# Splitting h later, loading h behind the weights, and adding the down evictions on VectorE: one step of a hybrid encoder layer

## The chip, the cores and the metric

The kernel runs on one core of a Trainium2 chip. The metric is the device time of one execution in microseconds, the median of the runs shown. A core has TensorE (PE; PEld is its weight load), VectorE (DVE), ScalarE (ACT), GpSimd (POOL) and SyncE (SP); DMAs are issued from the queues of SP, ACT and POOL and run on 16 DMA engines that these share.

## The reference

One encoder layer for a prompt of 512 frames with 16 meta tokens and for a decode step of 64 frames; from the residual on, 512 + 64 = 576 tokens are computed together. Width 2048, hidden width of the feed-forward part 5632, all in float32:

```python
h = h + concat([pool_mixer(u), diff_attention(q, k, v)]) @ w_out     # u, q, k, v = rmsnorm(h) @ w_in
n = rmsnorm(h, g_ffn)
h = h + (silu(n @ w_gate) * (n @ w_up)) @ w_down                     # the part that the change touches
y = rmsnorm(h, g_final)
```

## The kernel before

Activations are kept transposed, features on the 128 partitions and tokens along the free dimension. Every float32 matmul is made of three: each operand is split into a high part in float32r (a ScalarE copy) and a low part (a VectorE subtraction of the high part from the original), and high x high, high x low and low x high are accumulated (L808 to L810).

**Seven products.** Gate, up and down are done in blocks of two by two (two halves of the features in, two of the features out, or of the tokens: TN = 288), with seven products in place of eight. An object of class `Seven` holds one such step: `load` brings four raw weight blocks on SP's queue (L786), `prep(i)` forms the i-th combination of them on VectorE (L793 to L797) and splits it (L837, L838 for gate and up; L1070, L1071 for down), `product(i)` runs its matmuls into one of three PSUM banks A, B, C and calls the eviction. Several products use one bank after another: a bank's second product continues to accumulate on the first, so it must wait until the first one's eviction has read the bank. `run` (L814) traces, ahead of each product, the preparation of the product three steps later.

**Gate and up.** There are 22 pairs f, each a gate step and an up step of 7 x 8 x 3 = 168 matmuls. `inner` evicts (L864 to L880): ScalarE copies the first product out, VectorE adds the others; the last gate product accumulates into bank B, whose earlier content L873 reads at i = 4. After the last up product (i = 6) GpSimd forms the combinations of h that the down products need (L908 to L911). Then h[f], seven blocks of 128 x 288, is split in two portions, blocks 0 to 3 and 4 to 6: hi by ScalarE (L917, one buffer in tag "xlast"), the low part by VectorE in place (L918), hi stored to DRAM by a DMA from POOL's queue after each portion (L919), and the low part stored for all seven blocks at once (L920). The last f is stored whole and not split (L913).

**Down.** 40 turns: five passes r of eight output tiles m, each turn one `Seven` over up to five f's (2 to 5 in the first pass, 5 in the middle ones, 5 to 2 in the last). Products go in the order 1, 0, 2, 4, 3, 5, 6. The h of an f comes back in four loads (f, q) on SP's queue (L988): q = 0, 1, 2 are pairs of blocks (tile hc), q = 3 is the seventh block (tile hh). The weights of turns 0 and 1 (EARLY = 2) come early, those of turn 2 are loaded by `down[EARLY].load()`. After each product `hooks` takes one load from a list in order of f and q if a place is free. Loads of f >= 3 that are taken in turns 0 and 1 are ordered behind turn 2's weights with `issue_after`, which sets an order within one queue and no wait. `down_evac` evicts a product into y or a1 in SBUF: in pass 0 mostly by a ScalarE copy; later products 0, 3 and 6 by a ScalarE copy to a tile ev (L1087) and a DMA from POOL's queue that adds ev to its target (L1088), the others by a VectorE addition (L1090).

**What sets the order.** The tile framework traces the program and then a planner writes each engine's queue, by its own costs of the instructions; an engine works its queue strictly in that order. `issue_after` is how the program asks for an order. Tiles of one tag share their buffers in turn.

Of the kernel before, what the change touches and what calls it, by code (L numbers as in the profile page):

```python
# [11 lines left out]
F32 = mybir.dt.float32  # L12
F32R = mybir.dt.float32r
AF = mybir.ActivationFunctionType
ALU = mybir.AluOpType
# [4 lines left out]
P = 128  # L20
# [30 lines left out]
def hymba_step(  # L51
# [6 lines left out]
    nc = tc.nc  # L58
# [476 lines left out]
    for h in range(HEADS):  # L535
        hd = Head(h)
# [138 lines left out]
    TN = NQ // 2  # L675
# [3 lines left out]
    fs = ffb.enter_context(tc.tile_pool(name="fs", bufs=1, reuse_waits="tile"))  # L679
# [173 lines left out]
    hd = [dram.tile([P, 7, 2 if j < FT // 2 - 1 else 1, TN], F32, name=f"hd{j}") for j in range(FT // 2)]  # L853

    def inner(s, i, out, scale):


        A, B, C = s.b
        tt = nc.vector.tensor_tensor
        o11, o12, o21, o22, o2 = out  # L860
        if i == 0:
            pu = fs.tile([P, 2, TN], F32, name="pu", tag="acc")
            s.p1, s.u2 = pu[:, 0], pu[:, 1]
            nc.scalar.activation(s.p1, A, AF.Copy)  # L864
        elif i == 1:
            tt(s.u2, B, s.p1, op=ALU.add)
        elif i == 2:
            s.t5 = fs.tile([P, TN], F32, name="t5", tag="pre")
            tt(s.t5, C, s.p1, op=ALU.add)
        elif i == 3:  # L870
            tt(o11, A, scale[:, 0, 0], op=ALU.mult)
        elif i == 4:
            tt(o22, B, s.t5, op=ALU.add)  # L873
        elif i == 5:
            tt(o12, C, s.u2, op=ALU.add)
        else:
            tt(o21, B, s.p1, op=ALU.add)
        if i == 6:
            nc.gpsimd.tensor_tensor(o12, o12, scale[:, 0, 1], op=ALU.mult)
            nc.gpsimd.tensor_tensor(o2, o2, scale[:, 1], op=ALU.mult)  # L880

    def blocks(t):
        return t.rearrange("p i (c t) -> p i c t", c=2)

    def gate_evac(f):
        def evac(s, i):
            if i < 3:
                return inner(s, i, (None,) * 5, None)
            if i == 3:
                gates[f] = fw.tile([P, 2, NQ], F32, name="g")  # L890
            g = gates[f]
            rpb = rp[:, None, :].to_broadcast([P, 2, NQ])
            gb = blocks(g)
            inner(s, i, (gb[:, 0, 0], gb[:, 0, 1], gb[:, 1, 0], gb[:, 1, 1], gb[:, 1]), blocks(rpb))
            if i == 6:
                nc.scalar.activation(g, g, AF.Silu)
                nc.gpsimd.tensor_tensor(g, g, rpb, op=ALU.mult)
        return evac

    def up_evac(f):  # L900
        def evac(s, i):
            if i == 0:
                s.ho = fw.tile([P, 7, TN], F32, name="ho")
            h = s.ho
            inner(s, i, (h[:, 0], h[:, 6], h[:, 3], h[:, 5], h[:, 3:6:2]), blocks(gates[f]))
            if i == 6:
                tt = nc.gpsimd.tensor_tensor
                tt(h[:, 2], h[:, 6], h[:, 0], op=ALU.subtract)  # L908
                tt(h[:, 1], h[:, 5], h[:, 2], op=ALU.subtract)
                tt(h[:, 4], h[:, 5], h[:, 6], op=ALU.subtract)  # L910
                tt(h[:, 6], h[:, 3], h[:, 1], op=ALU.subtract)  # L911
                if f == FT // 2 - 1:
                    nc.gpsimd.dma_start(out=hd[f][:, :, 0], in_=h)  # L913
                    return
                for q, w in ((0, 4), (4, 3)):
                    hi = fs.tile([P, 4, TN], F32R, name="hi", tag="xlast")
                    nc.scalar.activation(hi[:, :w], h[:, q:q + w], AF.Copy)  # L917
                    nc.vector.tensor_tensor(h[:, q:q + w], h[:, q:q + w], hi.bitcast(F32)[:, :w], op=ALU.subtract)  # L918
                    nc.gpsimd.dma_start(out=hd[f][:, q:q + w, 0], in_=hi.bitcast(F32)[:, :w])  # L919
                nc.gpsimd.dma_start(out=hd[f][:, :, 1], in_=h)  # L920
        return evac

    def xs_ffn(i, j):
# [3 lines left out]
    for f in range(FT // 2):  # L927
        for src, evac in ((w_gate, gate_evac(f)), (w_up, up_evac(f))):
            first = not seq
            raws = first_raw if first else (lambda n: fw.tile([P, 8, P], F32, name="raw", bufs=5))  # L930
            tmp = (lambda: ext.tile([P, 8, P], F32, name="wrawt", tag="ext")) if first else \
                (lambda: fw.tile([P, 8, P], F32, name="wt"))
            psum = (lambda: banks(pz, "mm", "mm")) if src is w_gate else (lambda: banks(pj, "pj", "pj"))
            seq.append(Seven(src[0], 0, 8, f * 2 * P, raws, tmp, split_halves, xs_ffn, psum, evac))
# [24 lines left out]
    first_use = {f: min(n for n, (m, f0, f1) in enumerate(turns) if f0 <= f < f1) for f in range(NFP)}  # L959
    ACTS, HCS, HALF = KT, 5, (5, 3)  # L960
    END = (NR * 5, 0)
    hc, queue = {}, [(f, q) for f in range(NFP) for q in range(4)]
    now, taken = [(0, -1)], {"act": [(0, -1)] * ACTS, "hc": [END] * HCS}

    def slot_free():
        return min(min(t) for t in taken.values()) <= now[0]
# [18 lines left out]
    def h_operand(f, q):  # L985
        w, t = 2 if q < 3 else 1, h_slot(f, q)
        if f < NFP - 1:
            nc.sync.dma_start(out=t.bitcast(F32), in_=hd[f][:, 2 * q:2 * q + w])  # L988
            return
        for i in range(w):  # L990
            s = dw.tile([P, TN], F32, name="ev", tag="ev", bufs=4)
            nc.sync.dma_start(out=s, in_=hd[f][:, 2 * q + i, 0])
            nc.scalar.activation(t[:, i, 0], s, AF.Copy)
            nc.vector.tensor_tensor(t[:, i, 1], s, t.bitcast(F32)[:, i, 0], op=ALU.subtract)

    EARLY = 2
# [53 lines left out]
    def h_free(f, q, n, i):  # L1050
        if q == 3:
            return f < sum(HALF) or (last_use[f - sum(HALF)], 6) <= (n, i)
        return slot_free()

    def hooks(n, i):
        now[0] = (n, i)
        while queue and queue[0] in hc:
            queue.pop(0)
        if queue and h_free(*queue[0], n, i):
            later = n < EARLY and queue[0][0] >= 3  # L1060
            with tc.issue_after(down[EARLY].loaded.ins) if later else ExitStack():
                h_operand(*queue.pop(0))
        for f, q in queue:
            assert (f, q) in hc or first_use[f] > n or (first_use[f] == n and (0, 2, 3, 6)[q] > i), (f, q, n, i)
        finished(n, i)
# [10 lines left out]
    def down_evac(n, m):  # L1076
        r, y, s1 = n // NR, yt[m], a1[:, m]
        cp, tt = nc.scalar.activation, nc.vector.tensor_tensor

        def evac(s, i):  # L1080
            ps = s.b[(0, 1, 2, 0, 1, 2, 1)[i]]
            out = (s1, y[:, 1], y[:, 3], y[:, 0], y[:, 3], y[:, 1], y[:, 2])[i]
            if r == 0 and i not in (4, 5):
                copied[:] = [cp(out, ps, AF.Copy)]
            elif i in (0, 3, 6) and r < 4 or i in (3, 6) and m < 6:
                e = dw.tile([P, TN], F32, name="ev", tag="ev", bufs=4)
                cp(e, ps, AF.Copy)  # L1087
                nc.gpsimd.dma_start(out=out, in_=e, accum_op=ALU.add)  # L1088
            else:
                tt(out, ps, out, op=ALU.add)  # L1090
            if r == 4 and i == 0:
                nc.gpsimd.tensor_tensor(y[:, 1:4], y[:, 1:4], s1[:, None, :].to_broadcast([P, 3, TN]), op=ALU.add)
            if r == 1 and i == 6:
                nc.gpsimd.dma_start(out=y, in_=hres[m].rearrange("p i (c t) -> p (i c) t", c=2), accum_op=ALU.add)
        return evac
# [38 lines left out]
    def finished(n, i):  # L1134
        if n == 4 and i == 6:
            with tc.issue_after(copied[0].ins):
                nc.scalar.activation(stat[:, 0, 15:16], eps, AF.Sqrt)
        if n > len(turns) - NR and i == 5:
            rows_out(turns[n - 1][0])

    down = []
# [13 lines left out]
    def hrow(m):  # L1155
        return yt[m // 2].rearrange("p (i c) t -> p i (c t)", i=2)[:, m % 2]

    run(down, hooks, done=7 * EARLY, order=ORDER)
    rows_out(NR - 1)
    ms, sd, r, a = (stat[:, :, 8 + i] for i in range(4))  # L1160
# [58 lines left out]
```

## Time and profile before

| | |
|---|---|
| runs, us | 2377.16 median of 3 (2376.78 to 2377.47) |
| profiled execution, us | 2379.16; its span 2377.4 |
| granted TensorE clock | 0.986 |
| busy, us: PE / DVE / ACT / POOL | 2272.0 / 1851.6 / 1128.5 / 541.2 |
| gate and up, about 793 to 1819 us | 22 steps of each, some 46 us a pair |
| down, about 1819 to 2353 us | 40 turns |

How to read the profile's lines: times are us from the span's start. In a row of the order of time stand start, length, engine, line, operation, tiles (out<-in) and shape, and in brackets how long the engine was idle before and on whom it waited. A wait row reads: engine, tile and line <- releaser: total us, times, longest us. A row of a group gives the count, then busy us and the mean ns of one. A row of windows gives start and end, then for each engine its busy us and count, at the end the granted clock, the share of the DMA engines and GB/s.

### The profile page before, as it was taken

How to read it: one execution, taken by the hardware profiler on the slowest of the kernel's cores; microseconds unless marked ns; L12 is line 12 of the kernel's file. 1: busy time of each engine (PE TensorE's matmuls, PEld its weight loads, DVE VectorE, ACT ScalarE, POOL GpSimd, SP SyncE). 2: the span in 40 equal slices, each digit the busy share in tenths (PEclk: the TensorE clock that was granted, in tenths of full speed). 3: DMA queues.
4: the chain of work that ended last, by engine and by line, in shares of the span. 5: the costliest groups of instructions: out<-in, count | busy, mean ns of one | idle time of the engine just before them, and what ended most of it. 6: DMA issues, size and time to landing. Idle time of an engine off the chain costs nothing.

```text
span 2377.4 us, 43444 instructions
## 1 busy us (share of the span) xinstructions
PE 2272.0 (96%) x16815; PEld 2242.4 (94%) x16815; DVE 1851.6 (78%) x3424; ACT 1128.5 (47%) x2377; POOL 541.2 (23%) x503
## 2 busy tenths in 40 slices
PE   7999999999999799999999999999998899999995
PEld 6999999999999799999999999999998899999995
DVE  6888888765576988888888888788886677677787
ACT  5666666643344544444444444344444444344443
POOL 1000000002325123223232323232232012111222
PEclk9999999999999999999999999999999999999998
DMA  6433333223234344444544444344448589878743
GB/s 172 110 95 95 96 103 92 73 81 91 80 93 126 91 129 149 136 137 125 160 124 124 143 140 133 115 154 138 133 134 281 155 240 236 237 204 234 178 95 111
DMA packets 434193, 329.35 MB, mean 139 GB/s; under 512 B 13795, under 2 KB 404253, under 8 KB 433988
## 3 DMA queue, kind: packets, MB, share of 16 engines
q1 hardware_dynamic: 403616, 248.17, 35.3%
q0 software_dynamic: 29536, 76.98, 12.5%
q8 instruction: 132, 2.16, 0.4%
q10 hardware_dynamic: 836, 1.43, 0.2%
q14 instruction: 73, 0.60, 0.1%
HBM read 255.33 MB, written 62.03 MB: 133 GB/s over the span
## 4 chain that ended last, share of the span: by engine, by line
PE 67%; DVE 15%; DMA 5%; issue 5%; POOL 4%; ACT 3%; SPq 0%; ACTq 0%; DVEq 0%; POOLq 0%
PE pj L810 9%; PE pj L808 9%; PE pj L809 9%; PE pj L112 6%; PE pj L114 5%; PE pj L113 5%; DVE ws L838 5%; PE mm L808 4%; PE mm L810 4%; PE mm L809 4%; PE mm L114 3%; PE mm L112 3%; PE mm L113 3%; DMA hd<-hi 2%; DMA raw<-in_w_down_dram 2%
## 5 line engine op out<-in xcount | busy, mean ns | idle before, releaser
L837 ACT ACTIVATE ws<-raw 128x512 fp32r<-128x512 f32 x430 | 256.8, 627 | 340.1 <-DVE raw L795 145.1
L838 DVE TENSOR_TENSOR ws<-raw,ws 128x512 fp32r<-128x512 f32 x430 | 367.5, 890 | 50.5 <-ACT ws L837 50.1
L808 PE MATMUL mm<-xc,ws 128*128 128x288 f32 x1232 | 369.5, 300 | 38.5 <-DVE g L873 31.1
L808 PE MATMUL pj<-xc,ws 128*128 128x288 f32 x1232 | 364.8, 296 | 3.1 <-ACT ws L837 3.1
L809 PE MATMUL mm<-xc,ws 128*128 128x288 f32 x1232 | 365.8, 297 | 0.0
L810 PE MATMUL mm<-xc,ws 128*128 128x288 f32 x1232 | 364.1, 296 | 0.2 <-DVE ws L838 0.2
L810 PE MATMUL pj<-xc,ws 128*128 128x288 f32 x1232 | 362.5, 294 | 1.3 <-DVE ws L838 1.3
L809 PE MATMUL pj<-xc,ws 128*128 128x288 f32 x1232 | 362.9, 295 | 0.0
L112 PE MATMUL pj<-x,ws 128*128 128x296 f32 (+1 forms) x1024 | 317.7, 311 | 9.8 <-ACT x L106 8.5
L113 PE MATMUL pj<-x,ws 128*128 128x296 f32 (+1 forms) x1024 | 307.0, 300 | 0.0
L114 PE MATMUL pj<-x,ws 128*128 128x296 f32 (+1 forms) x1024 | 305.5, 299 | 0.0
L808 PEld LDWEIGHTS mm<-xc,ws 128*128 128x128 f32 x1232 | 234.3, 190 | 43.6 <-issue 35.7
L810 PEld LDWEIGHTS mm<-xc,ws 128*128 128x128 f32 x1232 | 235.4, 191 | 0.4 <-DVE ws L838 0.4
L809 PEld LDWEIGHTS mm<-xc,ws 128*128 128x128 f32 x1232 | 235.3, 191 | 0.1
L808 PEld LDWEIGHTS pj<-xc,ws 128*128 128x128 f32 x1232 | 231.9, 188 | 3.3 <-ACT ws L837 3.3
L810 PEld LDWEIGHTS pj<-xc,ws 128*128 128x128 f32 x1232 | 232.9, 189 | 1.6 <-DVE ws L838 1.6
L809 PEld LDWEIGHTS pj<-xc,ws 128*128 128x128 f32 x1232 | 232.8, 189 | 0.0
L137 ACT ACTIVATE ws<-wraw,vcols 128x128 fp32r<-128x128 f32 x512 | 169.4, 392 | 107.4 <-PE pj L114 87.7
L112 PEld LDWEIGHTS pj<-x,ws 128*128 128x128 f32 x1024 | 193.1, 189 | 14.9 <-ACT x L106 9.3
L1070 ACT ACTIVATE ws<-raw 128x640 fp32r<-128x640 f32 (+3 forms) x190 | 130.0, 687 | 147.0 <-DVE raw L795 52.1
L113 PEld LDWEIGHTS pj<-x,ws 128*128 128x128 f32 x1024 | 193.9, 189 | 0.4
L114 PEld LDWEIGHTS pj<-x,ws 128*128 128x128 f32 x1024 | 193.0, 188 | 0.0
(368 smaller groups left out, 5795.2 us busy)
## 6 DMA issues: line engine op xcount, KB each, us to landing
raw<-in_w_up_dram SPq DMA_DIRECT2D x88, 512.0 KB, 3.8
raw<-in_w_gate_dram SPq DMA_DIRECT2D x84, 512.0 KB, 4.5
hc<-hd SPq DMA_DIRECT2D x63, 576.0 KB, 8.0
raw<-in_w_down_dram SPq DMA_DIRECT2D x112, 320.0 KB, 5.0
wraw<-in_w_in_dram SPq DMA_DIRECT2D x64, 512.0 KB, 4.1
hd<-ho POOLq DMA_DIRECT2D x22, 1008.0 KB, 5.5
wraw<-in_w_out_dram SPq DMA_DIRECT2D x32, 512.0 KB, 4.0
hd<-hi POOLq DMA_DIRECT2D x21, 576.0 KB, 3.6
```

Of the source, the lines that this page charges most:

```text
L112: nc.tensor.matmul(ps, lhsT=w(0), rhs=x(0), start=first, stop=False)
L113: nc.tensor.matmul(ps, lhsT=w(0), rhs=x(1), start=False, stop=False)
L114: return nc.tensor.matmul(ps, lhsT=w(1), rhs=x(0), start=False, stop=last)
L137: nc.scalar.activation(ws[:, 0, k, :], r[:, k, :], AF.Copy, scale=g)
L808: nc.tensor.matmul(ps, lhsT=w(0), rhs=x(0), start=first and j == 0, stop=False, skip_group_check=True)
L809: nc.tensor.matmul(ps, lhsT=w(0), rhs=x(1), start=False, stop=False, skip_group_check=True)
L810: mm = nc.tensor.matmul(ps, lhsT=w(1), rhs=x(0), start=False, stop=j == self.nj - 1, skip_group_check=True)
L837: nc.scalar.activation(ws[:, 0], src[:, k:k + WK], AF.Copy)
L838: nc.vector.tensor_tensor(ws[:, 1], src[:, k:k + WK], ws.bitcast(F32)[:, 0], op=ALU.subtract)
L1070: nc.scalar.activation(ws[:, 0], src, AF.Copy)
```

## The change

Three edits. The split of h is no longer traced right behind the up step's last product: the two portions are noted in a list, and the next gate step traces them, the first behind its product 2 and the second behind its product 5 (`h_parts`). Each portion now stores its hi and its low part, so the low part goes out in two DMAs. In `hooks`, a load of h is taken only from three turns ahead of its first use on, and every load behind (2, 1) is ordered behind the last weight load of the next turn (turn 2 at the earliest). In `down_evac`, products 0, 3 and 6 of passes 1 to 3 are added by VectorE from PSUM; a copy and an adding DMA remain in pass 4, products 3 and 6, for six of the eight tiles.

```diff
--- before.py
+++ after.py
@@ -882,16 +882,33 @@
     def blocks(t):
         return t.rearrange("p i (c t) -> p i c t", c=2)
 
+    unsplit = []
+
+    def h_parts():
+        if unsplit:
+            f, h, q0, q1 = unsplit.pop(0)
+            hi = fs.tile([P, 4, TN], F32R, name="hi", tag="xlast")[:, :q1 - q0]
+            lo = h[:, q0:q1]
+            nc.scalar.activation(hi, lo, AF.Copy)
+            nc.vector.tensor_tensor(lo, lo, hi.bitcast(F32), op=ALU.subtract)
+            nc.gpsimd.dma_start(out=hd[f][:, q0:q1, 0], in_=hi.bitcast(F32))
+            nc.gpsimd.dma_start(out=hd[f][:, q0:q1, 1], in_=lo)
+
     def gate_evac(f):
         def evac(s, i):
             if i < 3:
-                return inner(s, i, (None,) * 5, None)
+                inner(s, i, (None,) * 5, None)
+                if i == 2:
+                    h_parts()
+                return
             if i == 3:
                 gates[f] = fw.tile([P, 2, NQ], F32, name="g")
             g = gates[f]
             rpb = rp[:, None, :].to_broadcast([P, 2, NQ])
             gb = blocks(g)
             inner(s, i, (gb[:, 0, 0], gb[:, 0, 1], gb[:, 1, 0], gb[:, 1, 1], gb[:, 1]), blocks(rpb))
+            if i == 5:
+                h_parts()
             if i == 6:
                 nc.scalar.activation(g, g, AF.Silu)
                 nc.gpsimd.tensor_tensor(g, g, rpb, op=ALU.mult)
@@ -911,13 +928,8 @@
                 tt(h[:, 6], h[:, 3], h[:, 1], op=ALU.subtract)
                 if f == FT // 2 - 1:
                     nc.gpsimd.dma_start(out=hd[f][:, :, 0], in_=h)
-                    return
-                for q, w in ((0, 4), (4, 3)):
-                    hi = fs.tile([P, 4, TN], F32R, name="hi", tag="xlast")
-                    nc.scalar.activation(hi[:, :w], h[:, q:q + w], AF.Copy)
-                    nc.vector.tensor_tensor(h[:, q:q + w], h[:, q:q + w], hi.bitcast(F32)[:, :w], op=ALU.subtract)
-                    nc.gpsimd.dma_start(out=hd[f][:, q:q + w, 0], in_=hi.bitcast(F32)[:, :w])
-                nc.gpsimd.dma_start(out=hd[f][:, :, 1], in_=h)
+                else:
+                    unsplit[:] = [(f, h, 0, 4), (f, h, 4, 7)]
         return evac
 
     def xs_ffn(i, j):
@@ -1056,9 +1068,9 @@
         now[0] = (n, i)
         while queue and queue[0] in hc:
             queue.pop(0)
-        if queue and h_free(*queue[0], n, i):
-            later = n < EARLY and queue[0][0] >= 3
-            with tc.issue_after(down[EARLY].loaded.ins) if later else ExitStack():
+        if queue and first_use[queue[0][0]] <= n + 3 and h_free(*queue[0], n, i):
+            ahead = down[max(min(n + 1, len(down) - 1), EARLY)]
+            with tc.issue_after(ahead.loaded.ins) if queue[0] > (2, 1) else ExitStack():
                 h_operand(*queue.pop(0))
         for f, q in queue:
             assert (f, q) in hc or first_use[f] > n or (first_use[f] == n and (0, 2, 3, 6)[q] > i), (f, q, n, i)
@@ -1082,7 +1094,7 @@
             out = (s1, y[:, 1], y[:, 3], y[:, 0], y[:, 3], y[:, 1], y[:, 2])[i]
             if r == 0 and i not in (4, 5):
                 copied[:] = [cp(out, ps, AF.Copy)]
-            elif i in (0, 3, 6) and r < 4 or i in (3, 6) and m < 6:
+            elif r == 4 and i in (3, 6) and m < 6:
                 e = dw.tile([P, TN], F32, name="ev", tag="ev", bufs=4)
                 cp(e, ps, AF.Copy)
                 nc.gpsimd.dma_start(out=out, in_=e, accum_op=ALU.add)
```

## The prediction

> **What bounds the kernel now.** I read the granted clock first, then the busy shares, then TensorE's waits by stage, and last the queues in order of time around those waits.
>
> ```profile
> core 0: 2377.4 us, clock 0.986
> PE 2272.0 (96%) x16815; PEld 2242.4 (94%) x16815; DVE 1851.6 (78%) x3424; ACT 1128.5 (47%) x2377; POOL 541.2 (23%) x503
> ```
>
> TensorE is busy for 96% of the span, so only its gaps and its slow stretches can be won. The list of waits for TensorE alone, over the gate and up stage (775 to 1815 us) and then over the down stage (1800 us to the end), gives name, total, count and longest:
>
> ```profile
> PE mm L808 <- DVE g L873: 31.1, 22, 3.1
> ```
>
> ```profile
> PE mm L808 <- ACT ws L1070: 7.6, 3, 4.8
> PE pj L808 <- ACT ws L1070: 3.8, 1, 3.8
> ```
>
> The table of windows adds what was lost to the clock (last columns: granted clock, DMA share, GB/s):
>
> ```profile
> 1200.00:1300.00 100.00, 96.86 (x720) 96.44 (x720) 83.50 (x111) 42.91 (x70) 29.34 (x24) 0.98 0.43 132
> 1300.00:1400.00 100.00, 96.14 (x715) 95.73 (x714) 82.18 (x108) 42.22 (x70) 30.20 (x25) 0.98 0.43 132
> 1500.00:1600.00 100.00, 95.43 (x701) 95.02 (x701) 81.37 (x105) 41.69 (x70) 29.74 (x25) 0.97 0.44 135
> 1800.00:1900.00 100.00, 88.88 (x629) 88.00 (x628) 62.08 (x100) 44.52 (x90) 9.70 (x9) 0.93 0.69 232
> 2000.00:2100.00 100.00, 96.35 (x704) 95.91 (x703) 69.82 (x103) 40.50 (x66) 19.80 (x23) 0.97 0.88 235
> 1905.00:2235.00 330.00, 323.71 (x2399) 321.00 (x2398) 235.48 (x347) 142.07 (x235) 63.61 (x74) 0.99 0.85 224
> 800.00:1815.00 1015.00, 979.30 (x7316) 974.05 (x7315) 853.63 (x1112) 446.39 (x733) 316.33 (x255) 0.99 0.45 137
> ```
>
> A clock of 0.98 over 100 us is 2 us of lost pulses: in gate and up 2 + 2 + 3 = 7 us, so that stage can give back 31.1 + 7 = 38 us at most. At the start of down it is 7.6 + 3.8 = 11.4 us of waits and 7 us of clock; around 2041 us, 3.4 and 3 us. These are the only stocks that the change can draw on.
>
> **Part 1, the split of h.** One period of VectorE and its effect (start, length, in brackets the idle time before and its releaser; the PE rows are from TensorE's order of time):
>
> ```profile
> 1220.26 1.36 DVE L918 TENSOR_TENSOR ho<-ho,hi 128x1152 f32<-128x1152 f32 x1 [2.36 <-POOL ho L911]
> 1225.91 1.06 DVE L918 TENSOR_TENSOR ho<-ho,hi 128x864 f32<-128x864 f32 x1 [2.13 <-ACT hi L917]
> 1234.16 0.45 DVE L873 TENSOR_TENSOR g<-mm,t 128x288 f32<-128x288 f32 x1
> 1234.76 0.58 PE L808 MATMUL mm<-xc,ws 128*128 128x288 f32 x1 [2.32 <-DVE g L873]
> ```
>
> And of the period before, which is the common kind:
>
> ```profile
> 1179.01 1.06 DVE L918 TENSOR_TENSOR ho<-ho,hi 128x864 f32<-128x864 f32 x1 [0.99 <-ACT hi L917]
> 1187.85 0.37 PE L808 MATMUL mm<-xc,ws 128*128 128x288 f32 x1 [1.19 <-DVE g L873]
> ```
>
> VectorE stands 2.36 us for GpSimd's combinations and then 0.99 or 2.13 us for the second hi; TensorE's wait at the gate's last product is that second wait plus 0.2 us (0.99 gives 1.19, 2.13 gives 2.32). If both halves really went behind L869 and L875, 2.36 + 0.99 us of idling and the second subtraction's 1.06 us would leave the path to L873, more than 1.2 us, and the wait would vanish. But the diff only moves the lines in the program; it adds no order edge for them. Do queues follow the program or readiness? GpSimd's order of time and the views of two lines (durations, then first and last start) in the output projection answer:
>
> ```profile
> 554.38 0.75 POOL L642 DMA_DIRECT2D wpr<-in_w_pool_dram  x1 [99.28 <-DVE mx L107]
> 555.56 0.52 POOL L607 DMA_DIRECT2D stt<-in_state_pool_dram  x1 [0.42 <-DVE stt L606]
> ```
>
> ```profile
> L645 DVE TENSOR_TENSOR wps<-wpr,wps x4: 682/684/692, 558.3 to 665.9; 128x512 fp32r<-128x512 f32 x4
> L600 DVE TENSOR_TENSOR hp<-mm,hp x64: 442/457/459, 567.1 to 783.2; 128x288 f32<-128x288 f32 x64
> ```
>
> L642 and L645 are traced at the tenth product of the loop, yet stand ahead of L607, which is traced before the loop, and of L600, which belongs to the first product. So the planner fills a queue by readiness, and the place in the program only breaks ties. In the h period nothing else is ready when the halves are: ScalarE's next copy (L864) waits for the gate's first product, VectorE's next split waits for a weight copy behind it, and L793 waits for the split after the second half. I therefore take the order, and the 22 waits, as unchanged: 0 us, with -38 us as one end. Should the cover fail the other way, the price is the second wait's, 1 us of TensorE for each us; see the third rival.
>
> The store of the low half becomes two, 21 more issues on GpSimd's queue. I price each at the 0.97 us of one issue now, 20 us in all, on an engine 23% busy whose next work in the period comes late:
>
> ```profile
> 1180.60 0.97 POOL L920 DMA_DIRECT2D hd<-ho  x1 [0.58 <-issue]
> 1189.87 1.18 POOL L879 TENSOR_TENSOR g<-g,rp 128x288 f32<-128x288 f32 x1 [8.30 <-DVE g L875]
> ```
>
> The 8.30 us of idling there cover it: 0 us. ScalarE's and VectorE's counts stay.
>
> **Part 2, h's loads.** SyncE's order of time at the start of down with the wait that it makes, the same around 2041 us, and the row of the weight loads (KB each, median us to landing):
>
> ```profile
> 1818.39 0.38 SPq L988 DMA_DIRECT2D hc<-hd  x1
> 1818.83 3.55 SPq L988 DMA_DIRECT2D hh<-hd  x4
> 1822.47 2.83 SPq L786 DMA_DIRECT2D raw<-in_w_down_dram  x4
> 1832.30 0.56 DVE L793 TENSOR_TENSOR wt<-raw 128x384 f32<-128x384 f32 x1 [2.31 <-DMA raw<-in_w_down_dram]
> 1834.89 0.61 PE L808 MATMUL mm<-hc,ws 128*128 128x288 f32 x1 [4.83 <-ACT ws L1070]
> ```
>
> ```profile
> 2030.72 5.05 SPq L988 DMA_DIRECT2D hh<-hd  x1
> 2039.85 0.83 DVE L793 TENSOR_TENSOR wt<-raw 128x640 f32<-128x640 f32 x1 [6.12 <-DMA raw<-in_w_down_dram]
> 2041.19 0.58 PE L808 MATMUL mm<-hc,ws 128*128 128x288 f32 x1 [3.45 <-DVE y L1090]
> ```
>
> ```profile
> raw<-in_w_down_dram SPq DMA_DIRECT2D x112, 320.0 KB, 5.0
> ```
>
> Turn 2's weights are issued at 1822.47 behind five h loads that turns 0 and 1 don't need; VectorE gets them at 1832.30, 9.8 us later, where a weight load takes 5.0 us in the median. The change puts what follows h(2,1) behind these weights, and its bound on first use keeps the loads of f = 4 and later out of the first turns. Issue can move up by as much as 1822.47 - 1818.4 = 4 us, landing by 9.8 - 5.0 = 4.8 us: 8.8 us against a wait of 4.83, so that wait goes, with about 1.7 us of half clock behind it (a quarter of the 7 us). What is late next is turn 3's weights, which are freed by turn 2's preparation; of the remaining 11.4 - 4.8 = 6.6 us I take back 2.5. Sum 9 us, between 0 (the issue waits for memory that the gate stage frees, not for h) and 11.4 + 7 = 18 us. Around 2041 us the loads of two f's, freed together, are spread by the bound over two turns; of 3.4 + 3 us I take 5. Behind the now ordered h loads stand the weights of the turn after; the h data are wanted two or three turns of 14 us later, so I add no wait, but one late h load would cost up to 8 us, the other end.
>
> By the Trainium skill, "DMA: Bandwidth & Descriptors", section "Queues, rings and completion order", descriptors of one queue are consumed in ring order on each DMA engine. The 9.8 us of the weights behind h loads agree with that; a load put ahead would then wait for no h at all, and the sum would go to the 18 us end.
>
> **Part 3, the evictions.** Of 2 x 42 copies (42 on each of the two sets of banks) 72 go, i in 0, 3, 6 in three passes of eight turns, each with its adding DMA on GpSimd's queue, and 72 adds of 0.451 us come:
>
> ```profile
> L1087 ACT ACTIVATE ev<-pj 128x288 f32<-128x288 f32 x42 | 17.2, 410 | 44.0 <-PE pj L810 43.9
> L1090 DVE TENSOR_TENSOR y<-mm,y 128x288 f32<-128x288 f32 x74 | 33.3, 451 | 9.7 <-PE mm L810 8.8
> ```
>
> That is 72 x 0.451 = 32.5 us for VectorE in turns 8 to 31, about 1905 to 2235 us, where it is idle for 330 - 235.5 = 94.5 us. It becomes 81% busy, below the 853.6 / 1015 = 84% of gate and up. Cost 0 us; 32.5 us if all of it lay on the path, which the idle time excludes but for single turns. ScalarE's 72 x 0.410 = 29.5 us and GpSimd's issues were off the path: no gain.
>
> **Sum.** The profiled execution took 2379.16 us, 1.8 us around its span, and 2.0 us above the median of 2377.16. 0 - 9 - 5 + 0 = -14 us: 2379.2 - 14 = 2365.2, and against the median 2363 us.
>
> **The rivals.** First, the split does move. Ties in the planner could fall otherwise once a second store of low halves is in its queue; against it stand the rows of L642 and L645. The 38 us go too: 2363 - 38 = 2325 us, or some 2344 if half the waits go. By the Trainium skill, "TensorE: Matmul & The Clock Gate", section "What's actually happening", the clock falls after an idle window of about 3.4 us; here the chain's pieces at 1235 us show half rate after a wait of 2.32 us, against the full rate at 1189 us after 1.19 us, so the trace disagrees; by the rule this rival would be 7 us weaker.
>
> ```profile
> 1235.34 0.24 PE mm L809
> ```
>
> ```profile
> 1189.01 0.14 PE mm L809
> ```
>
> Second, the change does not do what it says anywhere: the weights wait for memory and not for h, and the split stays: 2377 us. For it, SyncE's 0.38 us issues at 1822.47 show no wait of their own; I can't see when these slots came free.
>
> Third, slower: the low half's first store starts right behind the hi store, while the second hi waits for that hi store to land (its 576 KB take 3.6 us in the median) in a single buffer.
>
> ```profile
> hd<-hi POOLq DMA_DIRECT2D x21, 576.0 KB, 3.6
> ```
>
> If sharing makes it land half as late again, 1.8 us, TensorE waits 21 x 1.8 = 38 us longer: 2363 + 38 = 2401 us. It decides from 14 / 21 = 0.7 us a store. Against it: the store is issued only after the subtraction, over 1 us behind. By the same section of "DMA: Bandwidth & Descriptors" in the Trainium skill both stores stand in one ring and start in order, which would give this rival no delay; no row here shows two such stores together.
>
> **How the numbers follow.** My forecast (order kept, loads help) has 0.60, with its own range of 2352 to 2374 us; the split moving 0.18; no effect 0.11; the late store or another slip, such as an h load behind a weight load, 0.11. A measurement can tell about 0.2%, 4.8 us, so faster means below 2372.4. Of the forecast's 0.60 some 0.03 lie above that: faster 0.57 + 0.18 = 0.75, same 0.11 + 0.03 = 0.14, slower 0.11. A range of 2326 to 2378 us leaves out some 0.07 below and 0.12 above.
>
> **What would show it.** Right: L918 still preceded by 2.4 us for POOL and TensorE still waiting 22 times, some 31 us, for L873; the wait of 4.83 us near 1835 and that of 3.45 near 2041 gone, with the clock of 1800 to 1900 us nearer 0.97; L1087 x12 in all, L1090 x220, VectorE near 81% in 1905 to 2235 without new waits of TensorE for it. Wrong: L918 behind L869 or later in VectorE's order, hi landing later than 3.6 us, or TensorE waiting for hc or for L1090 in turns 8 to 31.

## The result and the profile after

The changed kernel takes 2362.03 us (median of 4 runs, 2359.36 to 2367.47), the kernel before 2377.31 us beside it (4 runs): ratio 0.9939, 95% interval 0.9921 to 0.9957. The forecast was 2363. The profiled execution is the slowest of the four, 2367.47 us with a span of 2365.7, so its difference to the profiled execution of before (2379.16 us) is 11.7 us where the medians differ by 15.3.

The new lines shift the numbers: h's subtraction is L893 (was L918), its copy L892, its stores L894 and L895, GpSimd's combinations L925 to L928, h's loads L1000 (was L988), down's weight split L1082 and L1083 (L1070 and L1071), the eviction's copy L1099 (L1087), its add L1102 (L1090).

Busy shares and TensorE's waits (775 to 1815 us, then 1800 us to the end; total, count, longest) of the changed kernel:

```profile
PE 2269.8 (96%) x16815; PEld 2241.8 (95%) x16815; DVE 1881.1 (80%) x3496; ACT 1105.2 (47%) x2305; POOL 491.0 (21%) x452
```

```profile
PE mm L808 <- DVE g L873: 31.3, 22, 3.0
```

```profile
PE mm L808 <- DVE y L1102: 6.2, 5, 2.6
PE pj L808 <- DVE y L1102: 3.7, 3, 2.2
PE pj L808 <- ACT ws L1082: 3.0, 1, 3.0
PE mm L808 <- ACT ws L1082: 0.9, 1, 0.9
```

The gate's 22 waits are all there, 31.3 us where they were 31.1. Down's waits for weights fell from 11.4 to 3.9 us. The windows of the changed kernel (TensorE, its loads, VectorE, ScalarE, GpSimd, then clock, DMA share, GB/s):

```profile
1800.00:1900.00 100.00, 95.86 (x694) 94.73 (x694) 66.78 (x106) 48.04 (x98) 11.16 (x9) 0.97 0.76 240
1905.00:2235.00 330.00, 326.73 (x2447) 325.85 (x2447) 269.75 (x424) 123.11 (x172) 6.91 (x8) 0.99 0.66 194
```

At the start of down TensorE gains 7.0 us of busy time per 100 and the clock goes from 0.93 to 0.97. In 1905 to 2235 us VectorE works 34.3 us more, the DMA share falls from 0.85 to 0.66, and TensorE is busy for 3.0 us more of these 330, so it idles less. To see where the time went, here is the last long wait of down in before, and in after the first wait for weights and the last long one (start, length, in brackets the wait; the first one of before, 4.83 us at 1834.89, stands in the prediction):

```profile
2352.68 0.37 PE L808 MATMUL pj<-hc,ws 128*128 128x288 f32 x1 [2.21 <-DVE y L1090]
```

```profile
1833.78 0.41 PE L808 MATMUL mm<-hc,ws 128*128 128x288 f32 x1 [0.91 <-ACT ws L1082]
2341.41 0.37 PE L808 MATMUL pj<-hc,ws 128*128 128x288 f32 x1 [2.20 <-DVE y L1102]
```

From the start of the first weight wait of down to the start of this last one, before needs (2352.68 - 2.21) - (1834.89 - 4.83) = 520.4 us and after (2341.41 - 2.20) - (1833.78 - 0.91) = 506.3 us: the gain, 14.1 us, lies between them. This execution came to the first of them 2.8 us later than that of before, which is why it shows 11.7 in all; 2.2 of these are there before VectorE splits h for the first time (854.3 us against 852.1).

### The profile page after: what moved, and what is told of

It reads as the page before. It is cut to its first block, busy times and chain, and to the rows that moved or that the text cites. A ratio compares the mean times of both kernels' runs of the same rounds, so it can differ in the third digit from the quotient of the medians.

```text
span 2365.7 us, 43325 instructions
## 1 busy us (share of the span) xinstructions
PE 2269.8 (96%) x16815; PEld 2241.8 (95%) x16815; DVE 1881.1 (80%) x3496; ACT 1105.2 (47%) x2305; POOL 491.0 (21%) x452
## 5 line engine op out<-in xcount | busy, mean ns | idle before, releaser
L808 PE MATMUL mm<-xc,ws 128*128 128x288 f32 x1232 | 369.6, 300 | 38.7 <-DVE g L873 31.3
L1082 ACT ACTIVATE ws<-raw 128x640 fp32r<-128x640 f32 (+3 forms) x190 | 130.2, 688 | 205.6 <-DVE raw L795 71.9
```

The costliest lines, as they stand in the source:

```text
L808: nc.tensor.matmul(ps, lhsT=w(0), rhs=x(0), start=first and j == 0, stop=False, skip_group_check=True)
L1082: nc.scalar.activation(ws[:, 0], src, AF.Copy)
```

## The experiments

The theory after the result: part 1 does nothing, because no edge orders the moved lines; part 2 brings the gain; part 3 brings nothing. The rivals: part 1 helps or harms and another part hides it; part 3 brings some of the gain. Where a ratio is given, it is to the kernel before, run beside it.

**e1, part 1 alone.** The kernel before with `h_parts` and its two calls, and nothing else of the diff.

> The kernel before with the new place of the split of h alone. Theory (the planner fills queues by readiness, so the new place in the program changes nothing): 2377 us, from 2374 to 2380; VectorE's subtraction of the low half still waits 2.36 us for GpSimd, TensorE still waits 22 times, some 31 us in all, for L873. Rival (the first low store delays the hi store's landing by up to 1.8 us): 22 waits of some 70 us in all and 2400 to 2415 us. Rival (the split does move): waits for L873 near zero and 2339 us.

Measured: 2379.78 us (10 runs), ratio 1.0005, interval 0.9996 to 1.0014. Its TensorE waits in 775 to 1815 us and its VectorE in order of time:

```profile
PE mm L808 <- DVE g L873: 31.2, 22, 3.0
```

```profile
1178.43 1.36 DVE L893 TENSOR_TENSOR ho<-ho,hi 128x1152 f32<-128x1152 f32 x1 [2.36 <-POOL ho L928]
1182.95 1.06 DVE L893 TENSOR_TENSOR ho<-ho,hi 128x864 f32<-128x864 f32 x1 [1.00 <-ACT hi L892]
```

The subtraction still stands for 2.36 us for GpSimd and then 1.00 us for the second hi, as before. Part 1 is worth nothing, and two low stores in place of one cost nothing, within the interval of -1 to +3 us.

**e2, part 2 alone.** The kernel before with the bound on first use and the order behind the next turn's weights.

> The kernel before with the new order and bound of h's loads alone. Theory (the loads carry the whole gain): 2363 us, from 2359 to 2367; the wait of 4.83 us at the third turn of down falls to about 1 us and that of 3.45 us near 2041 us goes or shrinks. Rival (the evictions carry it, since their adding DMAs share the DMA engines with the weights): at most a third of the gain, 2372 us or more, DMA share in the middle of down still about 0.85.

Measured: 2365.23 us (5 runs), ratio 0.9953, interval 0.9939 to 0.9966, a gain of 12.9 us of medians. The window at the start of down, the waits for weights, and the wait that stood at 2041 us:

```profile
1800.00:1900.00 100.00, 96.23 (x715) 94.76 (x714) 67.98 (x109) 49.76 (x101) 9.33 (x8) 1.00 0.80 254
```

```profile
PE pj L808 <- ACT ws L1070: 2.4, 1, 2.4
PE mm L808 <- ACT ws L1070: 1.1, 2, 0.9
```

```profile
1999.38 0.37 PE L808 MATMUL mm<-hc,ws 128*128 128x288 f32 x1 [2.97 <-DVE y L1090]
```

TensorE is busy 96.23 us in place of 88.88 and the clock is full; the waits for weights are 3.5 us in place of 11.4. The wait around 2041 us is not gone: it stands at 1999 us with 2.97.

**e3, part 3 alone.** The kernel before with the new condition for evictions.

> The kernel before with the new evictions alone. Theory (off the path on both sides): 2377 us, from 2374 to 2380; the wait of 4.83 us at the third turn of down stays, TensorE gets no new wait for VectorE in turns 8 to 31, where VectorE rises from 71 to 81 per cent busy. Rival (the removed adding DMAs free the DMA engines, share 0.85 to about 0.66): the wait near 2041 us and the short ones go, 2368 to 2372 us. Rival (VectorE's adds hold up the next turn's weights): 2382 us or more.

Measured: 2373.16 us (11 runs), ratio 0.9976, interval 0.9966 to 0.9987. This is small, some 5.7 us by the ratio, but the interval excludes that nothing was gained. The median lies between the range of the theory (2374 to 2380) and that of the first rival (2368 to 2372). The theory put 0 here; this is the part of it that fell. The product of the two single ratios, 0.9953 x 0.9976 = 0.9929, lies inside the interval of the whole change.

**e4, the split with order edges.** The changed kernel, with the two halves really ordered behind the products that the text of the program puts them behind:

```
-            nc.scalar.activation(ws[:, 0], src[:, k:k + WK], AF.Copy)
+            copied_w[:] = [nc.scalar.activation(ws[:, 0], src[:, k:k + WK], AF.Copy)]
...
-            tt(s.t5, C, s.p1, op=ALU.add)
+            added[:] = [tt(s.t5, C, s.p1, op=ALU.add)]
...
-            tt(o12, C, s.u2, op=ALU.add)
+            added[:] = [tt(o12, C, s.u2, op=ALU.add)]
...
+            with tc.issue_after(copied_w[0].ins), tc.issue_after(added[0].ins):
                 nc.scalar.activation(hi, lo, AF.Copy)
                 nc.vector.tensor_tensor(lo, lo, hi.bitcast(F32), op=ALU.subtract)
```

> The changed kernel with order edges for the split: each portion's hi copy behind ScalarE's last traced weight copy and its subtraction behind VectorE's addition of gate product 2 or 5. Theory (the path to L873 is shortened by 2.36 + 0.99 us of idling and 1.06 us of work, more than the wait): all 22 waits go with their 7 us of half clock, 2362 - 38 = 2324 us, from 2319 to 2332. Rival (the first subtraction still stands ahead of L873 and the new place brings waits of its own): half of it, 2344 us. Rival (the waits for L873 are set by VectorE's total work in the gate step and not by its idling): no change, 2362 us.

Measured: 2325.74 us (4 runs), ratio 0.9779, interval 0.9765 to 0.9792: 38 us below the changed kernel by the two ratios. VectorE's idle time before the subtraction, by releaser (us, times), first in the changed kernel:

```profile
L893 DVE TENSOR_TENSOR ho<-ho,hi x42: 1057/1209/1361, 854.3 to 1786.8; 128x1152 f32<-128x1152 f32 x21, 128x864 f32<-128x864 f32 x21
...
  POOL ho L928: 49.5, 21
  ACT hi L892: 28.3, 21
```

Then in e4, where it is L894, VectorE's order of time, what is left of TensorE's waits for L873 in 775 to 1800 us, and the window of the gate and up stage:

```profile
1170.41 0.45 DVE L869 TENSOR_TENSOR t<-mm,pu 128x288 f32<-128x288 f32 x1
1170.78 1.35 DVE L894 TENSOR_TENSOR ho<-ho,hi 128x1152 f32<-128x1152 f32 x1
```

```profile
PE mm L808 <- DVE g L873: 0.2, 1, 0.2
```

```profile
800.00:1800.00 1000.00, 994.82 (x7500) 993.30 (x7499) 897.28 (x1140) 464.65 (x760) 351.06 (x283) 1.00 0.49 147
```

The subtraction follows L869 without a gap, VectorE no longer idles for GpSimd or ScalarE there, TensorE's 22 waits for L873 are down to one of 0.2 us, and it is busy 994.8 us of 1000. The granted clock is 1.00 in every window of 100 us from 900 us on; from 800 to 900 it is 0.95 (0.98 in before), behind a wait of 3.07 us for weights at 826.76 that comes ahead of the first split. So the 38 us that the prediction counted as that stage's whole stock exist and can be had; the change left them where they were only for want of an edge.

**e5 and e6, the halves of part 2.** e5 has only the bound, e6 only the order:

```
e5:
-        if queue and h_free(*queue[0], n, i):
+        if queue and first_use[queue[0][0]] <= n + 3 and h_free(*queue[0], n, i):
e6:
-            later = n < EARLY and queue[0][0] >= 3
-            with tc.issue_after(down[EARLY].loaded.ins) if later else ExitStack():
+            ahead = down[max(min(n + 1, len(down) - 1), EARLY)]
+            with tc.issue_after(ahead.loaded.ins) if queue[0] > (2, 1) else ExitStack():
```

> The kernel before with one half of the change to the loads of h: a load is issued only for a chunk used within three turns; the order behind the weights stays as it was (h of chunk 3 and later, in turns 0 and 1, behind turn 2's weights). Theory: the gain of the loads part (12.9 us with both halves, 2365.2 against 2378.1) comes from the order, so this half alone gives little: 2374 to 2379, the first wait of down's start stays between 3 and 5 us. Rival: keeping the early h loads off the queue is what lets the weights through, so this half gives most of the gain: 2365 to 2368 and a first wait of about 1 us.

> The kernel before with the other half: every load of h past chunk 2's second part is issued behind the next turn's weights (turn 2's at the earliest), with no bound on how far ahead h is loaded. Theory: 2364 to 2368, with waits of about 0.9 and 3 us at down's start, as with both halves. Rival (the bound carries it): 2374 to 2379, with the first wait still above 3 us.

Measured: e5 2373.69 us (12 runs), ratio 0.9983, interval 0.9972 to 0.9993; e6 2373.33 us (11 runs), ratio 0.9982, interval 0.9973 to 0.9990. Neither theory nor rival: each half gives some 4 us, and only both together 12.9. The longest waits for weights at the start of down, e5 first, e6 then:

```profile
1836.09 0.61 PE L808 MATMUL mm<-hc,ws 128*128 128x288 f32 x1 [7.44 <-ACT ws L1070]
```

```profile
1832.37 0.40 PE L808 MATMUL mm<-hc,ws 128*128 128x288 f32 x1 [0.91 <-ACT ws L1070]
1851.66 0.61 PE L808 MATMUL pj<-hc,ws 128*128 128x288 f32 x1 [10.69 <-ACT ws L1070]
```

With the bound alone, h loads still go ahead of turn 2's weights (7.44 us); with the order alone, turn 2's weights go first and a crowd of h loads goes ahead of turn 3's (10.69 us). So with one half alone the queue stays jammed at one turn or the other. Where each half gains is another matter, and the windows of the middle of down (e5, then e6) and e6's wait near 2041 us show it:

```profile
1905.00:2235.00 330.00, 321.39 (x2394) 319.01 (x2392) 234.27 (x346) 141.43 (x235) 64.57 (x75) 0.99 0.85 221
```

```profile
1905.00:2235.00 330.00, 327.55 (x2455) 325.56 (x2454) 239.94 (x355) 146.19 (x243) 64.55 (x75) 1.00 0.87 229
```

```profile
2041.20 0.37 PE L808 MATMUL mm<-hc,ws 128*128 128x288 f32 x1 [1.11 <-DVE y L1090]
```

e5 gains at the start: its waits for weights there come to 8.7 us where before has 11.4, and the clock of 1800 to 1900 us is 0.97 in place of 0.93; in the middle TensorE is busy 2.3 us less than in before. e6 is worse at the start, 14.3 us of waits for weights, and gains in the middle, where TensorE is busy 3.8 us more than in before and the wait of 3.45 us near 2041 is 1.11.

**e7, e8, e9, where part 3's gain comes from.** Three ways to take apart "72 copies, 72 adding transfers" (in all three the last round stays as in the change; in e9 a tile of zeros takes the place of one of the four eviction buffers):

```
e7: copy to the buffer, VectorE adds from the buffer, no transfer
     cp(e, ps, AF.Copy)
-    nc.gpsimd.dma_start(out=out, in_=e, accum_op=ALU.add)
+    tt(out, e, out, op=ALU.add)
e8: VectorE adds from the accumulator, a plain transfer of the same bytes to a spare buffer
-    cp(e, ps, AF.Copy)
-    nc.gpsimd.dma_start(out=out, in_=e, accum_op=ALU.add)
+    tt(out, ps, out, op=ALU.add)
+    nc.gpsimd.dma_start(out=e, in_=out)
e9: VectorE adds from the accumulator, an adding transfer of zeros to the sum
-    cp(e, ps, AF.Copy)
-    nc.gpsimd.dma_start(out=out, in_=e, accum_op=ALU.add)
+    tt(out, ps, out, op=ALU.add)
+    nc.gpsimd.dma_start(out=out, in_=zeros, accum_op=ALU.add)
```

> The kernel before with the 72 evictions of down changed in another way: ScalarE still copies the product to a buffer, and VectorE adds from that buffer, so the adding transfers go but ScalarE's 72 copies stay. (In the last round of turns the transfers stay, as in the change.) Theory: the 5 us that the evictions part gained come from the transfers taken off the DMA engines, so this gains the same: 2371 to 2375, with a DMA share near 0.67 in 1905 to 2235 us. Rival 1: they come from ScalarE's 72 copies that went, so weights' copies start sooner: 2376 to 2380 here. Rival 2: an add from a buffer costs VectorE more or less than one from the accumulator, and VectorE becomes the wait: 2380 or more.

> The kernel before with VectorE adding from the accumulator as in the change, and with a transfer of the same size from the sum to an unused buffer behind each of the 72, so that the traffic stays and ScalarE's copies and the wait of the sum for the transfer's add go. Theory (traffic on the DMA engines): the gain is lost, 2376 to 2380, DMA share near 0.85 in 1905 to 2235 us. Rival 1 (ScalarE's copies): the gain stays, 2371 to 2375.

> The kernel before with VectorE adding 72 of down's products from the accumulator, as in the change, and with an adding transfer of the old kind and size kept behind each: it adds a tile of zeros to the sum, so ScalarE's copies go while the transfers' time on the DMA engines and the sum's wait for them stay. (The copy-out of the run before put back the bytes, but only 3456 of the 10368 packets and a DMA share of 0.77 where the adding transfers made 0.85.) Theory: the gain of about 5 us comes from the DMA engines' time and is lost here: 2376 to 2380, DMA share near 0.85 in 1905 to 2235 us. Rival (ScalarE's 72 copies): 2371 to 2375 with a DMA share near 0.85.

Measured: e7 2374.80 us (11 runs), ratio 0.9987, interval 0.9978 to 0.9996; e8 2372.13 us (11 runs), 0.9979, 0.9970 to 0.9987; e9 2381.01 us (11 runs), 1.0013, 1.0004 to 1.0022. What VectorE waited for weights in 1905 to 2235 us (total, count, longest), in before, e3, e7, e8 and e9, in this order:

```profile
DVE wt L793 <- DMA raw<-in_w_down_dram: 21.4, 9, 6.1
```

```profile
DVE wt L793 <- DMA raw<-in_w_down_dram: 13.4, 7, 5.7
```

```profile
DVE wt L793 <- DMA raw<-in_w_down_dram: 12.3, 5, 6.4
```

```profile
DVE wt L793 <- DMA raw<-in_w_down_dram: 14.0, 9, 4.0
```

```profile
DVE wt L793 <- DMA raw<-in_w_down_dram: 21.0, 9, 5.7
```

The two kernels that keep the adding transfers wait 21 us for weights, the three that dropped them 12 to 14, and only those three gain. TensorE follows in the same stretch: it is busy 323.7 us in before, 326.0, 325.2 and 327.9 in e3, e7 and e8, but 322.9 in e9. ScalarE's copies as the whole cause fall with e9, which has none of the 72 and is not faster than before but 3 us slower (it also has one eviction buffer fewer). e8 moves as many bytes as before and keeps the gain, at a DMA share of 0.77, so my expectation of 0.85 for it was wrong, and bytes are not what costs. GpSimd's queue in the same stretch (packets, MB, share of 16 DMA engines) in before, e3 and e8:

```profile
q0 software_dynamic: 10536, 14.34, 26.3%
```

```profile
q0 software_dynamic: 1152, 4.72, 7.9%
```

```profile
q0 software_dynamic: 4359, 14.58, 16.2%
```

Over e3 the adding transfers take 26.3 - 7.9 = 18.4% of the DMA engines' time, plain copies of the same bytes 16.2 - 7.9 = 8.3%. That their time is what delays the weights is inferred from these rows. That the sum itself must wait for its transfer is no cause in e9: in these passes VectorE touches the 72 sums in these adds only, and the releasers of its idle time before them (us, times) are all TensorE's.

```profile
  PE mm L810: 4.7, 12
  PE pj L810: 3.6, 9
```

One thing stays open: e7 has no adding transfers but keeps the copies, and its interval overlaps those of e3 and e8, so whether ScalarE's copies hold back a part of the gain is not settled. Nor does the gain lie in one wait of TensorE: the one near 2041 us, 3.45 in before, is 2.73 in e3, 3.75 in e7, 1.04 in e8 and 2.74 in e9.

**e10, the bound at two turns.** e4 with one number changed, `first_use[queue[0][0]] <= n + 2`.

> The changed kernel with the split of h ordered by edges (2325.7 us in its run), and the bound on h's loads at two turns in place of three. Theory: what is left of the third turn's wait in down (2.3 us here, 3.0 in the changed kernel) is h of a later chunk that goes ahead of turn 3's weights on SP's queue; behind this bound it comes later, the wait goes and the time is 2321 to 2324. Rival 1: those weights are late by their own transfer, no change: 2325 to 2328. Rival 2: h itself comes late for its turn: a new wait in down's start, 2328 or more.

Measured: 2321.74 us (4 runs), ratio 0.9763, interval 0.9749 to 0.9776, against 0.9765 to 0.9792 for e4. The time is in the theory's range, but the intervals overlap and the wait did not quite go. The start of down in e4 and in e10:

```profile
1803.38 0.40 PE L808 MATMUL pj<-hc,ws 128*128 128x288 f32 x1 [2.29 <-ACT ws L1083]
```

```profile
1807.44 0.40 PE L808 MATMUL mm<-hc,ws 128*128 128x288 f32 x1 [1.88 <-ACT ws L1083]
```

Turn 3's wait is gone, and turn 4's takes its place with 1.88 us, so this wait's part of the 4 us between the medians is 0.4 us. Of the 4.6 us between the two profiled executions 4.0 are there when ScalarE first copies a part of h (854.2 us against 858.2), and up to that point the two kernels are the same. e10 is the fastest kernel of this study, by a margin over e4 that these runs don't prove.

## Why the prediction was right, point by point

**Part 1, 0 us.** Right, by the reason given: for these lines the place in the program set nothing. e1 measures 1.0005, and e4 shows that an edge is what was missing. The stock of 38 us was sized about right: e4 gains 38 us over the changed kernel, give or take some 5 by the two intervals. By the Trainium skill, "TensorE: Matmul & The Clock Gate", section "What's actually happening", the clock falls after an idle window of about 3.4 us, and the stock would have been 31 us, since these waits are shorter (3.1 us at most). The clock disagrees: the three windows that stood at 0.97 to 0.98 are at 1.00 in e4, where the waits are gone; the 38 us alone would not decide it. The third rival is dead as well: with a low store behind it, the first hi still lands after the 3.6 us of before (the row of the changed kernel, median us in the last column). The second hi, of 432 KB, takes 4.5 us where it took 3.1, and the waits for L873 did not grow.

```profile
hd<-hi POOLq DMA_DIRECT2D x21, 576.0 KB, 3.6
```

**Part 2, -14 us.** Right in sum (e2 measures -12.9), wrong in its split. The start of down was to give 9 us, of 18.4 at most; in e2 it gave 11.4 - 3.5 = 7.9 us of waits and 7 us of clock, 14.9 in all. Around 2041 us I took 5 us, because the bound would spread the loads of two f's over two turns, and there the step failed. With the bound alone (e5) a wait of 3.58 us stays at 2035.76; with the order alone (e6) it is 1.11 us; with both it is moved, not removed, 2.97 us at 1999 us in e2 and 2.62 in the changed kernel, where SyncE shows a likely reason:

```profile
1993.58 2.36 SPq L1000 DMA_DIRECT2D hc<-hd  x1
1996.04 0.45 SPq L786 DMA_DIRECT2D raw<-in_w_down_dram  x1
```

```profile
2002.26 0.83 DVE L793 TENSOR_TENSOR wt<-raw 128x640 f32<-128x640 f32 x1 [5.56 <-DMA raw<-in_w_down_dram]
```

```profile
2003.59 0.37 PE L808 MATMUL mm<-hc,ws 128*128 128x288 f32 x1 [2.62 <-DVE y L1102]
```

The last weight block of a turn is still issued behind an hc load, which stands 2.4 us in the queue. The edge orders an h load behind the next turn's weights; it says nothing of the weights of the turn after, which come behind that load. That this load makes the wait is inferred. By e2's trace the start gave some 6 us more than the 9, and the rest of its 12.9 us, about -2, is 7 less than the 5. The two errors nearly cancel, and the 5.7 us of part 3 below stood nowhere in the sum (the single gains add up to more than the whole change's, within the intervals): that 2363 was met within 1 us is in part luck. The order of issue itself came out as said:

```profile
1822.57 0.45 DVE L877 TENSOR_TENSOR ho<-pj,pu 128x288 f32<-128x288 f32 x1
```

```profile
1817.76 3.41 SPq L1000 DMA_DIRECT2D hh<-hd  x2
1822.67 2.85 SPq L786 DMA_DIRECT2D raw<-in_w_down_dram  x4
```

```profile
1830.45 0.55 DVE L793 TENSOR_TENSOR wt<-raw 128x384 f32<-128x384 f32 x1
```

Turn 2's weights go out 0.1 us after the start of L877, the last eviction of the stage before; in before L877 started at 1818.79 and they went out 3.7 us behind it. So they moved up 3.6 of the 4 us allowed. SyncE now stands 1.8 us for VectorE ahead of them, so that the end that the memory sets (the second rival's point) is the bound there. (The 0.38 us that this rival read at 1822.47 is the row of the h load at 1818.39; the four weight issues took 2.83 us.) The landing moved up too. For the 3 us from their issue on, SyncE's queue (packets, MB, share of 16 DMA engines) and the four loads (KB each, median us to landing), in before and then in the changed kernel:

```profile
q1 hardware_dynamic: 497, 1.04, 97.8%
raw<-in_w_down_dram SPq DMA_DIRECT2D x4, 192.0 KB, 7.6
```

```profile
q1 hardware_dynamic: 555, 0.45, 46.7%
raw<-in_w_down_dram SPq DMA_DIRECT2D x4, 192.0 KB, 4.0
```

In before the queue moved more in these 3 us than the four loads hold (0.79 MB), and yet they landed only after 7.6 us: what it moved was in good part h. In the changed kernel they landed 3.6 us sooner, where I had counted 4.8. VectorE's row at 1830.45 shows no wait for them; it had stood until then for TensorE's products, whose evictions come first in its queue. What is late next is turn 3, as named, with 3.03 us.

**Part 3, 0 us.** Here a term was mis-sized: it measures about -5.7 us (e3). VectorE hid the adds as said (269.75 of 330 us, 82%, and L1102 x228 with L1099 x12; I had written 220 because I left out the eight adds of the other tile that were there before). What failed is the sentence that ScalarE's copies and GpSimd's issues "were off the path: no gain". The issues were: e8 keeps 72 of them and gains. The transfers behind them were not: by e7 to e9 the gain goes with them, and the way that I infer is that they share the DMA engines with the weights at a share of 0.85, and that a weight that lands late holds VectorE and then TensorE. For the copies it stays open. The table of windows had that share in its last columns, and the prediction quoted it without using it.

```profile
2000.00:2100.00 100.00, 96.04 (x715) 94.77 (x715) 77.62 (x123) 34.62 (x48) 2.42 (x3) 1.00 0.68 197
```

```profile
2040.63 0.37 PE L808 MATMUL mm<-hc,ws 128*128 128x288 f32 x1 [2.73 <-DVE y L1090]
```

This is e3: the wait at 2041 us is 2.73 in place of 3.45, and the clock stays at 1.00 where it fell to 0.97.

## What to carry to other kernels

Where a planner fills the queues, moving lines in the program can be no change at all until an order edge goes with it; look first whether anything forces the new place, and check it in the order of time of the engine. On a first-in queue, order and amount go together: the right order with an unbounded number of loads ahead jams the next turn, and a bound without the order jams this one. A transfer that nobody waits for isn't free when the DMA share is at 0.85 and the loads of the critical path use the same engines.

## What was not expected of the hardware

An SBUF to SBUF transfer that adds costs the DMA engines 18.4 / 8.3 = 2.2 times the time of a plain one of nearly the same bytes, in some 142 packets each (10536 - 1152 = 9384 over 66) against 48 (3207 over 67). And the clock's fall does not go by the length of a wait alone in these traces: in before the matmuls ran at half rate right behind a wait of 2.32 us (0.58 us for the first one at 1234.76), while in e3 they ran at the full rate behind 2.73 us (0.37 us at 2040.63), and the clock of 2000 to 2100 us is 1.00 there. The fall can also come late: in e5 the first matmuls behind a wait of 3.58 us ran at the full rate, and the half rate (0.44 us a matmul where it had been 0.29) began 1.5 us later:

```profile
2035.76 0.37 PE L808 MATMUL mm<-hc,ws 128*128 128x288 f32 x1 [3.58 <-DVE y L1090]
2037.27 0.44 PE L809 MATMUL mm<-hc,ws 128*128 128x288 f32 x1
```
